# RG-LRU gate products in quarters of TensorE, adaLN weights in half transfers, and a first norm without GpSimd

## The chip, the cores and the metric

The kernel runs on one core of a Trainium2 chip. The metric is the time of one execution on the device in microseconds (us); lower is better. A core has TensorE (PE: matmuls; PEld: its weight loads, which overlap the matmuls), VectorE (DVE), ScalarE (ACT), GpSimd (POOL) and SyncE (SP), which issues the transfers. Each engine takes its instructions strictly from its own queue and waits on semaphores for the others. Times come from the median of several executions; the rows come from one profiled execution.

## The reference

Two layers of a hybrid trunk over 512 tokens (256 context, 256 latent) of width 1024. In each layer, a modulated RMS norm, one input projection, three token mixers side by side (RG-LRU, chunked GLA, attention), a gated merge, an output projection, and an MLP. What the change touches is the modulated norm and the gates of the RG-LRU:

```python
def modulate(x, g, shift, scale):
    return rms_norm(x, g) * (1 + scale) + shift

def rglru_coeffs(xc, a_w, a_b, x_w, x_b, lam):
    bn, n, w = xc.shape
    xh = xc.reshape(bn, n, LRU_BLOCKS, LRU_BLOCK_W)
    r = jax.nn.sigmoid(jnp.einsum('bnhi,hij->bnhj', xh, a_w).reshape(bn, n, w) + a_b).astype(jnp.float32)
    i = jax.nn.sigmoid(jnp.einsum('bnhi,hij->bnhj', xh, x_w).reshape(bn, n, w) + x_b)
    log_a = -RGLRU_C * r * jax.nn.softplus(-lam.astype(jnp.float32))
    a = jnp.exp(log_a)
    u = jnp.sqrt(-jnp.expm1(2.0 * log_a)) * (i * xc).astype(jnp.float32)
    return a, u
```

`xc` is the projection after a convolution over four tokens. There are two directions with weights of their own, so four products (`a_w` and `x_w`, forward and reverse) for each of LRU_BLOCKS = 16 blocks of 64 channels. `shift` and `scale` come from `c_silu @ mod_w + mod_b` (adaLN), a product with a few columns of its own for context and latent tokens.

## The kernel before, in words

Activations lie channels on partitions: eight tiles of 128 channels by 512 tokens. A projection (`gemm`, L256) of one 128-column weight tile is 24 matmuls, as weights and activations are split in a high and a low fp32r part (`weight_parts`, L194: ACT casts `wh`, DVE subtracts `wl`); in layer 1 the projections of which only the latent half is used run on 256 columns. Weight tiles of 512 KB come through `weight_raw` (L189) into three buffers, the split parts into three more, so that a load waits until DVE has split the tile three before. Matmuls on plain fp32 operands show as two records in the trace, called two passes here.

**The start** (L453 to L484). `mod_load` (L381) fetches 2 MB of `mod_w`, a quarter of what the first norm needs, in one transfer; SyncE's order is quarter, two weight tiles, quarter, one weight tile, two quarters. `mod_half` / `mod_cols` (L313) make a quarter's product in 32 fp32 matmuls of 32 output columns, four on column tiles of their own (`ps[32 * j:32 * j + 32]`), then ACT copies, PE transposes and DVE adds the bias into `modT`. `norm_stats` (L397) sums squares, and PE broadcasts the inverse root to all partitions (L417, from diagonal tiles that DVE makes, L416) into PSUM `pb`, which ACT copies to `sb`. `norm_apply` (L429) multiplies each tile: even `k` on DVE from `pb`, odd `k` on GpSimd from `sb` (L439); scale and shift on DVE for `k` in `NDVE = (0, 2, 5)` (L446), on ACT for the others (L448); `split_to` (L306) casts on ACT (L307) and subtracts on DVE (L308). The first three projections go along with it, two `k` at a time.

**The RG-LRU stage** (L692 to L721). `gate_y` (L538) is a projection and a Gelu; `lru_conv` (L548) a projection, one ACT step and three DVE steps into `xc`; `lru_gates` (L558) four fp32 matmuls 128x128x512 with block-diagonal weights `gw` (256 KB, L561), each into a PSUM tile of its own from `ps_mx` (four buffers), a Tanh each (L567), and for each direction another Tanh (L571) and a DVE product (L572). `lru_decay` is Exp (L578), L710 a Sqrt over a pair of tiles, `lru_scan` DVE's scans and the split of the result. Tiles go in pairs; LYS gives the number of `gate_y` per step (2, 2, 1, 0 behind the first three):

```python
        for i in range(0, 8, 2):
            lru_conv(i + 1)
            if i < 6:
                lru_gates(i)
                lru_conv(i + 2)
            else:
                kq0 = gla_kq(0)
                lru_gates(i)
            lru_gates(i + 1)
            for j in range(2):
                lru_decay(i + j)
            tt = ws_[1][:, i % 4:i % 4 + 2]
            S.activation(tt, tt, AF.Sqrt, scale=0.25, bias=epsc)
            for j in range(LYS[l][i // 2 + 1]):
                gate_y(next(ly))
```

The program names an order, but the framework places each engine's instructions itself: by program order and priority among what is ready in its own model of the time (weight loads have a priority 800 instructions ahead). The queues are fixed by that before the kernel runs.

Of the kernel before, what the change touches and what calls it, by code (L numbers as in the profile page):

```python
# [15 lines left out]
F32 = mybir.dt.float32  # L16
# [8 lines left out]
T = 512  # L25
# [16 lines left out]
NDVE = (0, 2, 5)  # L42
NL = 2
O_LX, O_LY, O_GQ, O_GK, O_GV, O_GR, O_GZ = 0, 1024, 2048, 2560, 3072, 4096, 5120
# [60 lines left out]
def trunk_kernel(ctx: ExitStack, tc: tile.TileContext, out: bass.AP, d: dict):  # L105
    nc = tc.nc
    V, S, G, P = nc.vector, nc.scalar, nc.gpsimd, nc.tensor
# [11 lines left out]
    sm = ctx.enter_context(tc.tile_pool(name="sm", bufs=2))  # L119
# [21 lines left out]
    def mx():  # L141
        return ps_mx.tile([128, 512], F32, name="mx")
# [40 lines left out]
    x1 = load_x()  # L183
# [5 lines left out]
    def weight_raw(*key):  # L189
        r = wraw.tile([128, 1024], F32, name="wraw")  # L190
        nc.sync.dma_start(r, d["wt"][order[key]])
        return r
# [185 lines left out]
        yield pace  # L378
        turn()

    def mod_load(l, u, h, tag):  # L381

        t = yp.tile([128, KT, 2, 256], F32, name="modw", tag=tag)
        nc.sync.dma_start(t, d["mod_w"][l, u, h].rearrange("p k (h c) -> p k h c", h=2))
        return t

    def mod_half(l, u, h, t):
# [38 lines left out]
        h = hp.tile([128, KT, 2, T], F32R, name="h")  # L426
        return (h[:, :, 0, :], h[:, :, 1, :], a, g, h)

    def norm_apply(l, which, x, c0, c1, st, hn, ks):  # L429
        n = c1 - c0  # L430
        sh0, sc0 = (0, 8) if which == 1 else (24, 32)
        hh, hl, a, g = hn[:4]
        k0, k1, s0, s1 = ks[0], ks[-1] + 1, c0 // 256, c1 // 256
        V.scalar_tensor_tensor(a[:, k0:k1, s0:s1], modT[l][:, sc0 + k0:sc0 + k1, s0:s1], 1.0, g[:, k0:k1, s0:s1],
                               op0=ALU.add, op1=ALU.mult)
        for k in ks:
            h = tmp()
            if k % 2:
                G.tensor_tensor(h[:, :n], x[:, k, c0:c1], st[1][:, :n], op=ALU.mult)  # L439
            else:  # L440
                V.tensor_tensor(h[:, :n], x[:, k, c0:c1], st[0][:, :n], op=ALU.mult)
            for s in range(s0, s1):
                c = slice(256 * s - c0, 256 * s - c0 + 256)
                sc, sh = a[:, k, s:s + 1], modT[l][:, sh0 + k, s:s + 1]
                if k in NDVE:
                    V.tensor_scalar(h[:, c], h[:, c], sc, sh, op0=ALU.mult, op1=ALU.add)  # L446
                else:
                    S.activation(h[:, c], h[:, c], AF.Identity, scale=sc, bias=sh)  # L448
            split_to(hh[:, k, c0:c1], hl[:, k, c0:c1], h[:, :n])

    hn1 = norm_mul(0, 1)  # L453
    mq = [mod_load(0, 0, 0, "yh")]
    raw = [weight_raw(0, "in", O_LY + 128 * i) for i in range(2)]
    mq.append(mod_load(0, 0, 1, "yl"))
    raw.append(weight_raw(0, "in", O_LY + 256))
    mq += [mod_load(0, 1, h, ("yh", "yl")[h]) for h in range(2)]
    first_ps = [ps_mm.tile([128, 512], F32, name="mm") for _ in range(3)]

# [8 lines left out]
    st = norm_stats(x1, 0, between=lambda: next(gs[0]))  # L469
    run(gs[0])  # L470
    next(gs[1])
    norm_apply(0, 1, x1, 0, T, st, hn1, range(2))
    run(gs[1])
    first = [weight_parts(r) for r in raw]
    for q in range(4):
        first_gemm(0, q)
        if q < 2:
            next(gs[q + 2])
        if q < 3:
            norm_apply(0, 1, x1, 0, T, st, hn1, range(2 * q + 2, 2 * q + 4))  # L480
        first_gemm(1, q)
        if q < 2:
            run(gs[q + 2])
        first_gemm(2, q)  # L484
# [30 lines left out]
    for l in range(NL):  # L515
        last = l == NL - 1
        c0 = 256 if last else 0
        n0 = T - c0
        x = x1
# [18 lines left out]
        def gate_y(i):  # L538
            if l == 0 and i < 3:
                ps = first_ps[i]  # L540
            else:
                ps = gemm(weight(l, "in", O_LY + 128 * i, hi=E_LYH), hh, hl, c0)
            ge[i] = x[:, i, :256] if last else tmp()
            S.activation(ge[i], ps, AF.Gelu_apprx_tanh)

        xcs = {}

        def lru_conv(i):  # L548
            ps = gemm(weight(l, "in", O_LX + 128 * i, hi=E_LXH, lo=E_LXL, ahead=AHEAD if l or i > 1 else 0), hh, hl, 0)
            xc = xcs[i] = tmp()  # L550

            S.activation(xc, ps, AF.Identity, scale=pc(l, "cw", 8 + i, 1), bias=pc(l, "cb", i, 1))
            x3, p3 = (a.rearrange("p (s t) -> p s t", s=2) for a in (xc, ps))
            for k, (a, b) in ((0, (1, 256)), (2, (0, 255)), (3, (0, 254))):
                V.scalar_tensor_tensor(x3[:, :, a:b], p3[:, :, a + k - 1:b + k - 1], pc(l, "cw", 8 * k + i, 1),
                                       x3[:, :, a:b], op0=ALU.mult, op1=ALU.add)

        def lru_gates(i):  # L558
            xc = xcs.pop(i)
            gw = sm.tile([128, 4, 128], F32, name="gw")  # L560
            nc.sync.dma_start(gw, d["lruw"][l, i])  # L561
            rt, tt, ix = (t[:, i % 4] for t in ws_)
            for dd in range(2):
                for q, dst in ((0, rt), (1, ix)):
                    pg = mx()
                    P.matmul(pg, gw[:, 2 * dd + q, :], xc, start=True, stop=True)  # L566
                    S.activation(dst[:, dd, :], pg, AF.Tanh, scale=0.5,  # L567
                                 bias=habx[:, l, 16 * q + 8 * dd + i:16 * q + 8 * dd + i + 1])

                c2p = c2[:, l, 1, 8 * dd + i:8 * dd + i + 1]  # L570
                S.activation(tt[:, dd, :], rt[:, dd, :], AF.Tanh, scale=c2p, bias=c2p)  # L571
                V.scalar_tensor_tensor(ix[:, dd, :], ix[:, dd, :], 1.0, xc, op0=ALU.add, op1=ALU.mult)  # L572
# [117 lines left out]
        LYS = LYS0, LYS1  # L690
        ly = iter(range(8))
# [4 lines left out]
            gate_consts()  # L696
        for i in range(0, 8, 2):
            lru_conv(i + 1)
            if i < 6:
                lru_gates(i)  # L700
                lru_conv(i + 2)
            else:

                kq0 = gla_kq(0)
# [3 lines that stand above are left out]
                lru_decay(i + j)  # L708
            tt = ws_[1][:, i % 4:i % 4 + 2]
            S.activation(tt, tt, AF.Sqrt, scale=0.25, bias=epsc)  # L710
            for j in range(LYS[l][i // 2 + 1]):
                gate_y(next(ly))
            if i == 6:
                gates0 = gla_gates(0)
                v0 = gla_v(0)
            for j in range(2):
                lru_scan(i + j)
            if i == 6:
                ys0 = gla_r(0)
            if i == GZP:  # L720
                zs = gla_z()  # L721
# [399 lines left out]
def layout(inp):  # L1121
# [52 lines left out]
        put(l, "qg", A["q_norm_g"][l])  # L1174
        put(l, "kg", A["k_norm_g"][l])
    a["par"] = par
    lruw = np.zeros((NL, 8, 128, 4, 128), f)
    for dd in range(2):
        for q, name in enumerate(("lru_a_w", "lru_x_w")):
            w = A[name][:, dd].reshape(NL, 8, 2, 64, 64)  # L1180
            for s in range(2):
                lruw[:, :, 64 * s:64 * s + 64, 2 * dd + q, 64 * s:64 * s + 64] = w[:, :, s]
    a["lruw"] = lruw
    glaw = np.zeros((NL, 3, 32, 2, 512), f)
    for dd in range(2):
# [36 lines left out]
```

## Time and profile before

| | us |
|---|---|
| median of 3 runs | 1862.1 (1861.45 to 1863.89) |
| the profiled execution | 1860.73 |
| its span, first to last instruction | 1858.9 |
| mean granted TensorE clock | 0.993 |

Groups of rows give for each line of the kernel the engine, the operation, what it writes and reads (out<-in), and the shape (partitions x elements; for matmuls also rows*columns of the weights). In timelines the first number is the start from the span's begin and the second the time from the first start to the last end, both in us; instructions of one kind are merged (xcount), and square brackets hold the engine's idle time before them and what ended it. Matmuls are pipelined, so that their records overlap: the distance between starts is what one costs. A few records can be missing.

### The profile page before, as it was taken

The page shows a single profiled execution, that of the slowest core. Times are in us where ns is not written, and L with a number is a line of the kernel's source. Part 1 is how long each engine was busy: PE and PEld are TensorE (multiplying, and loading weights), DVE is VectorE, ACT ScalarE, POOL GpSimd, SP SyncE. Part 2 cuts the span into 40 slices and gives each one's busy share as a digit, 9 for nine tenths or more (in the row PEclk, how much of TensorE's full clock was granted, in tenths as well). Part 3 has the DMA queues.
Part 4 walks back from the last instruction along what each step waited for, and adds up shares of the span by engine and source line. Part 5 has one row for each costly group of instructions (what it writes and reads, how often), then busy time and mean ns, then how long its engine had stood idle before and what let it go on. Part 6 is the DMA issues. An engine that isn't in the chain of part 4 may idle for free.

```text
span 1858.9 us, 26345 instructions
## 1 busy us (share of the span) xinstructions
PE 1803.0 (97%) x9992; PEld 1496.2 (80%) x9992; DVE 1288.0 (69%) x2206; ACT 936.3 (50%) x1620; POOL 62.8 (3%) x87
## 2 busy tenths in 40 slices
PE   5999999999999999999999999999999999999999
PEld 4766788888787888988888889767889877878887
DVE  4786775454557777789763447797876588778776
ACT  4787545333444333564332325788665455556443
POOL 1000000000000000000000000000000000000000
PEclk9999999999999999999999999999999999999999
DMA  8322222232211556666753235522333432755554
GB/s 324 102 76 85 70 82 80 70 102 80 68 57 52 196 188 201 215 219 208 237 178 100 91 95 184 173 92 85 109 101 122 131 125 91 261 170 159 186 188 148
DMA packets 82143, 255.59 MB, mean 137 GB/s; under 512 B 9184, under 2 KB 12384, under 8 KB 81248
## 3 DMA queue, kind: packets, MB, share of 16 engines
q1 hardware_dynamic: 82016, 253.90, 42.0%
q8 instruction: 79, 1.29, 0.3%
q14 instruction: 48, 0.39, 0.1%
HBM read 252.82 MB, written 1.05 MB: 137 GB/s over the span
## 4 chain that ended last, share of the span: by engine, by line
PE 59%; issue 22%; DVE 9%; ACT 7%; POOL 1%; DMA 1%; SPq 0%; POOLq 0%; DVEq 0%; ACTq 0%
PE mm L216 48%; PE mx L216 5%; DVE wl L201 2%; PE mx L841 2%; ACT lru L567 1%; PE mx L220 1%; PE mx L822 1%; ACT wh L200 1%; ACT lru L710 1%; DVE lru L586 1%; PE mx L566 1%; DVE lru L588 1%; ACT lru L571 1%; PE mx L793 1%; DMA wraw<-wt 1%
## 5 line engine op out<-in xcount | busy, mean ns | idle before, releaser
L216 PE MATMUL mm<-h,wh 128*128 128x512 f32 (+1 forms) x2512 | 729.6, 370 | 7.1 <-ACT h L307 5.1
L200 ACT CAST wh<-wraw 128x1024 fp32r<-128x1024 f32 x365 | 382.2, 1049 | 500.9 <-PE mm L216 391.5
L201 DVE TENSOR_TENSOR wl<-wraw,wh 128x1024 fp32r<-128x1024 f32 x365 | 445.5, 1222 | 235.6 <-ACT wh L200 219.9
L216 PEld LDWEIGHTS mm<-h,wh 128*128 128x128 f32 x2512 | 452.4, 189 | 91.5 <-issue 7.2
L216 PE MATMUL mm<-h,wl 128*128 128x512 f32 (+1 forms) x1448 | 493.9, 341 | 0.0
L216 PEld LDWEIGHTS mm<-h,wl 128*128 128x128 f32 x1448 | 274.0, 189 | 31.6 <-issue 1.4
L216 PE MATMUL mm<-yh,wh 128*128 128x512 f32 (+1 forms) x640 | 224.7, 351 | 2.2 <-DVE big L1039 2.1
L216 PE MATMUL mm<-yh,wl 128*128 128x512 f32 (+1 forms) x640 | 224.0, 350 | 0.0
L216 PE MATMUL mm<-yl,wh 128*128 128x512 f32 (+1 forms) x640 | 222.4, 348 | 0.0
L216 PE MATMUL mm<-yp,wh 128*128 128x512 f32 (+1 forms) x576 | 183.6, 374 | 2.5 <-ACT g L873 2.3
L216 PE MATMUL mm<-wh,h 128*128 128x512 f32 x576 | 183.4, 395 | 0.0
L216 PE MATMUL mm<-yp,wl 128*128 128x256 f32 x512 | 145.1, 283 | 0.0
L370 DVE SCALAR_TENSOR_TENSOR t<-t,cs,t 128x512 f32<-128x512 f32 x178 | 127.2, 746 | 25.6 <-DMA t<-mod_w 18.7
L216 PEld LDWEIGHTS mm<-yh,wh 128*128 128x128 f32 x640 | 121.7, 190 | 17.4 <-issue 3.0
L216 PEld LDWEIGHTS mm<-yh,wl 128*128 128x128 f32 x640 | 121.2, 189 | 15.4 <-issue 0.7
L216 PEld LDWEIGHTS mm<-yl,wh 128*128 128x128 f32 x640 | 121.2, 189 | 14.9 <-issue 0.5
L216 PEld LDWEIGHTS mm<-wh,h 128*128 128x128 f32 x576 | 107.7, 188 | 23.1 <-issue 1.0
L216 PEld LDWEIGHTS mm<-yp,wh 128*128 128x128 f32 x576 | 104.1, 189 | 24.0 <-ACT g L873 2.5
L216 PE MATMUL mm<-wl,h 128*128 128x512 f32 x288 | 113.4, 394 | 0.0
L216 PEld LDWEIGHTS mm<-yp,wl 128*128 128x128 f32 x512 | 96.9, 189 | 0.8 <-issue 0.7
L216 PE MATMUL mx<-t,t 128*128 128x128 f32 (+2 forms) x416 | 81.7, 338 | 0.1
L989 ACT ACTIVATE t<-mx,mxs,rsq 128x512 f32<-128x512 f32 (+1 forms) x48 | 33.9, 709 | 74.0 <-DVE mxs L987 72.0
(223 smaller groups left out, 2006.5 us busy)
## 6 DMA issues: line engine op xcount, KB each, us to landing
wraw<-wt SPq DMA_DIRECT2D x365, 512.0 KB, 3.6
t<-mod_w SPq DMA_DIRECT2D x144, 256.0 KB, 3.5
modw<-mod_w SPq DMA_DIRECT2D x6, 2048.0 KB, 14.4
big<-xt SPq DMA_DIRECT2D x8, 512.0 KB, 5.1
gw<-lruw SPq DMA_DIRECT2D x16, 256.0 KB, 3.7
out<-big SPq DMA_DIRECT2D x8, 128.0 KB, 1.9
t<-glaw SPq DMA_DIRECT2D x8, 96.0 KB, 2.9
t<-ropeg SPq DMA_DIRECT2D x2, 256.0 KB, 3.3
```

The costliest lines, as they stand in the source:

```text
L200: S.copy(wh, r)
L201: (G if lo == "G" else V).tensor_tensor(wl, r, wh.bitcast(F32), op=ALU.subtract)
L216: P.matmul(o, a, b, **kw)
L220: P.transpose(o, a, ident)
L370: V.scalar_tensor_tensor(a, t, c, a, op0=ALU.mult, op1=ALU.add)
L566: P.matmul(pg, gw[:, 2 * dd + q, :], xc, start=True, stop=True)
L567: S.activation(dst[:, dd, :], pg, AF.Tanh, scale=0.5, bias=habx[:, l, 16 * q + 8 * dd + i:16 * q + 8 * dd + i + 1])
L571: S.activation(tt[:, dd, :], rt[:, dd, :], AF.Tanh, scale=c2p, bias=c2p)
L586: V.tensor_tensor(u, u, h, op=ALU.mult)
L588: V.tensor_tensor_scan(h, a, u, 0.0, op0=ALU.mult, op1=ALU.add)
L841: P.matmul(po[:, :256], a, b, start=j == 0, stop=j == len(mm) - 1)
L989: S.activation(p[:, :128 * nk], psc[:, :128 * nk], AF.Exp, scale=r, bias=mxs[:, 1:2], accum_out=mxs[:, 2:3])
```

## The change

Three things. `mod_load` issues two transfers of 1 MB (`k` 0 to 3, 4 to 7) with a callback between them, and the first weight tile is now issued between the halves of the second quarter, the other two behind it. `norm_apply` gets `on_g`; with False, as the first norm calls it, all multiplies are on DVE from PSUM and all scales and shifts on ACT. `lru_gates` uses 64x64 matmuls: `gw` holds the `a` blocks on partitions 0 to 63 and the `x` blocks on 64 to 127 (128 KB), and as each block of channels needs both, `lru_conv` makes a copy `xs` of `xc` with its halves swapped, by two transfers on SyncE, in a `g2` buffer. `gate_y` moves: half of a step's go behind `lru_conv(i + 1)`, ahead of the gates, the other half behind `lru_conv(i + 2)`.

```diff
-    def mod_load(l, u, h, tag):
+    def mod_load(l, u, h, tag, between=lambda: None):
         t = yp.tile([128, KT, 2, 256], F32, name="modw", tag=tag)
-        nc.sync.dma_start(t, d["mod_w"][l, u, h].rearrange("p k (h c) -> p k h c", h=2))
+        src = d["mod_w"][l, u, h].rearrange("p k (h c) -> p k h c", h=2)
+        nc.sync.dma_start(t[:, :4], src[:, :4])
+        between()
+        nc.sync.dma_start(t[:, 4:], src[:, 4:])
         return t
...
-            if k % 2:
+            if k % 2 and on_g:
                 G.tensor_tensor(h[:, :n], x[:, k, c0:c1], st[1][:, :n], op=ALU.mult)
...
-                if k in NDVE:
+                if k in NDVE and on_g:
                     V.tensor_scalar(h[:, c], h[:, c], sc, sh, op0=ALU.mult, op1=ALU.add)
...
-    mq = [mod_load(0, 0, 0, "yh")]
-    raw = [weight_raw(0, "in", O_LY + 128 * i) for i in range(2)]
-    mq.append(mod_load(0, 0, 1, "yl"))
-    raw.append(weight_raw(0, "in", O_LY + 256))
+    raw = []
+    mq = [mod_load(0, 0, 0, "yh"),
+          mod_load(0, 0, 1, "yl", lambda: raw.append(weight_raw(0, "in", O_LY)))]
+    raw += [weight_raw(0, "in", O_LY + 128 * i) for i in range(1, 3)]
...
+            xs = xss[i] = gtmp()
+            nc.sync.dma_start(xs[:64], xc[64:])
+            nc.sync.dma_start(xs[64:], xc[:64])
...
-            xc = xcs.pop(i)
-            gw = sm.tile([128, 4, 128], F32, name="gw")
+            xc, xs = xcs.pop(i), xss.pop(i)
+            gw = sm.tile([128, 2, 128], F32, name="gw")
...
             for dd in range(2):
+                pgs = mx(), mx()
+                for q in range(2):
+                    r = slice(64 * q, 64 * q + 64)
+                    for b in range(2):
+                        P.matmul(pgs[q][64 * b:64 * b + 64, :], gw[r, dd, 64 * b:64 * b + 64],
+                                 (xc if b == q else xs)[r, :], start=True, stop=True)
                 for q, dst in ((0, rt), (1, ix)):
-                    pg = mx()
-                    P.matmul(pg, gw[:, 2 * dd + q, :], xc, start=True, stop=True)
+                    pg = pgs[q]
...
             lru_conv(i + 1)
+            n = LYS[l][i // 2 + 1]
+            for j in range(0, n, 2):
+                gate_y(next(ly))
             if i < 6:
                 lru_gates(i)
                 lru_conv(i + 2)
+                for j in range(1, n, 2):
+                    gate_y(next(ly))
...
-            for j in range(LYS[l][i // 2 + 1]):
-                gate_y(next(ly))
```

## Rows read from the trace of the kernel before

**Rows 1.** The page: busy us of each engine, share of the span, instructions.

```profile
PE 1803.0 (97%) x9992; PEld 1496.2 (80%) x9992; DVE 1288.0 (69%) x2206; ACT 936.3 (50%) x1620; POOL 62.8 (3%) x87
```

**Rows 2.** Stretches: length, busy us per engine (instructions), granted clock, DMA share, GB/s.

```profile
63.00:172.00 109.00, 106.23 (x403) 74.97 (x402) 81.72 (x113) 84.37 (x110) 0.00 (x0) 0.98 0.27 86
1188.00:1213.00 25.00, 25.00 (x117) 18.47 (x116) 16.91 (x23) 23.74 (x30) 0.00 (x0) 1.00 0.36 119
1188.00:1285.00 97.00, 92.84 (x424) 66.52 (x423) 78.94 (x120) 84.44 (x114) 0.00 (x0) 1.00 0.30 97
```

**Rows 3.** Timeline of PE around one gates call of layer 0.

```profile
62.50 0.62 PE L216 MATMUL mm<-h,wh 128*128 128x512 f32 x2
62.95 0.39 PE L216 MATMUL mm<-h,wl 128*128 128x512 f32 x1
63.18 3.60 PE L566 MATMUL mx<-t,gw 128*128 128x512 f32 x8
```

**Rows 4.** The chain of work that ended last: start, us, what.

```profile
63.34 3.43 PE mx L566 x8
```

**Rows 5.** Timeline of the start: PE, GpSimd, DVE and ACT.

```profile
12.81 1.84 PE L409 MATMUL mx<-meanc,t 128*128 128x1 f32 x8 [12.81 <-DVE t L406]
...
16.81 1.04 ACT L200 CAST wh<-wraw 128x1024 fp32r<-128x1024 f32 x1 [5.46 <-DMA wraw<-wt]
...
18.07 1.05 ACT L200 CAST wh<-wraw 128x1024 fp32r<-128x1024 f32 x1 [0.21 <-DMA wraw<-wt]
...
19.36 2.08 PE L417 MATMUL mx<-t,ones 128*128 128x128 f32 x8 [0.17 <-DVE t L416]
...
22.10 0.69 DVE L441 TENSOR_TENSOR t<-big,mx 128x512 f32<-128x512 f32 x1 [0.19 <-ACT t L419]
22.14 5.04 POOL L439 TENSOR_TENSOR t<-big,t 128x512 f32<-128x512 f32 x4 [6.20 <-ACT t L419]
...
23.52 1.09 ACT L448 ACTIVATE t<-t,modT,amul 128x256 f32<-128x256 f32 x2 [1.46 <-DVE amul L434]
23.94 2.11 DVE L446 TENSOR_SCALAR t<-t,amul,modT 128x256 f32<-128x256 f32 x2
...
26.09 0.62 ACT L307 CAST h<-t 128x512 fp32r<-128x512 f32 x1 [0.82 <-DVE t L446]
...
26.76 0.79 PE L216 MATMUL mm<-h,wh 128*128 128x512 f32 x1 [5.12 <-ACT h L307]
...
27.48 3.64 PE L216 MATMUL mx<-modw,cs 128*32 128x128 f32 x64
...
32.69 0.74 DVE L446 TENSOR_SCALAR t<-t,amul,modT 128x256 f32<-128x256 f32 x2
```

**Rows 6.** Timeline of PE around the third adaLN quarter.

```profile
35.24 0.39 PE L216 MATMUL mm<-h,wl 128*128 128x512 f32 x1
...
35.56 1.96 PE L216 MATMUL mx<-modw,cs 128*32 128x128 f32 x64
...
37.45 0.73 PE L216 MATMUL mm<-h,wh 128*128 128x512 f32 x2
```

**Rows 7.** Timeline of ACT behind the first gates call.

```profile
68.61 1.28 ACT L578 ACT_TABLE_LOAD   x1
69.90 1.52 ACT L578 ACTIVATE lru<-lru,c 128x512 f32<-128x512 f32 x2
```

**Rows 8.** Timeline of PE and of ACT at layer 0's last gates call.

```profile
163.52 0.62 ACT L307 CAST yh<-lru 128x512 fp32r<-128x512 f32 x1 [3.55 <-DVE lru L595]
...
164.78 5.40 PE L566 MATMUL mx<-t,gw 128*128 128x512 f32 x8 [2.77 <-ACT lru L567]
```

**Rows 9.** Timeline of DVE: the three steps of the first conv.

```profile
59.94 2.31 DVE L555 SCALAR_TENSOR_TENSOR t<-mm,par,t 128x510 f32<-128x510 f32 x3
```

**Rows 10.** SyncE's waits from 52 to 236 us: total us, times, longest.

```profile
SPq L191 <- DVE wl L201: 143.3, 23, 9.6
```

**Rows 11.** The page, DMA issues: count, KB each, median us from issue to landing.

```profile
gw<-lruw SPq DMA_DIRECT2D x16, 256.0 KB, 3.7
```

More of the change, by code (lines that the diff above doesn't have):

```diff
@@ L427, in norm_mul, with norm_apply @@
         return (h[:, :, 0, :], h[:, :, 1, :], a, g, h)
-    def norm_apply(l, which, x, c0, c1, st, hn, ks):
+    def norm_apply(l, which, x, c0, c1, st, hn, ks, on_g=True):
         n = c1 - c0
@@ L471, in trunk_kernel @@
     next(gs[1])
-    norm_apply(0, 1, x1, 0, T, st, hn1, range(2))
+    norm_apply(0, 1, x1, 0, T, st, hn1, range(2), False)
     run(gs[1])
@@ L479, in trunk_kernel @@
         if q < 3:
-            norm_apply(0, 1, x1, 0, T, st, hn1, range(2 * q + 2, 2 * q + 4))
+            norm_apply(0, 1, x1, 0, T, st, hn1, range(2 * q + 2, 2 * q + 4), False)
         first_gemm(1, q)
@@ L544, in gate_y @@
             S.activation(ge[i], ps, AF.Gelu_apprx_tanh)
-        xcs = {}
+        xcs, xss = {}, {}
         def lru_conv(i):
@@ L1176, in layout @@
     a["par"] = par
-    lruw = np.zeros((NL, 8, 128, 4, 128), f)
+    lruw = np.zeros((NL, 8, 128, 2, 128), f)
     for dd in range(2):
@@ L1181, in layout @@
             for s in range(2):
-                lruw[:, :, 64 * s:64 * s + 64, 2 * dd + q, 64 * s:64 * s + 64] = w[:, :, s]
+                lruw[:, :, 64 * q:64 * q + 64, dd, 64 * s:64 * s + 64] = w[:, :, s]
     a["lruw"] = lruw
```

## The prediction

> **What bounds the kernel now.** I read the busy shares first [rows 1]: PE 97%, DVE 69%, ACT 50%. These are averages, so I cut out the two stages that the change touches most, the RG-LRU stages of layer 0 (63 to 172 us) and layer 1 (1188 to 1285 us), and read each engine's busy time there [rows 2]. PE is busy for 106.2 of 109 us and 92.8 of 97 us. ACT, 50% on average, is at 84.4 of 109 and 84.4 of 97 us here, and in layer 1's first pair of channel tiles at 23.7 of 25 us. DVE stands at 81.7 and 78.9 us. So PE sets the end of these stages, but ACT is close behind it, hardly any distance at all in layer 1. Whatever PE loses, ACT can give back only up to its own busy time.
>
> Then the PE timeline around one gates call [rows 3]: behind projection matmuls, which start 0.227 us apart (three between 62.50 and 63.18), stand eight gate passes, four fp32 matmuls of two passes each. The chain of work that ended last has them at 3.43 us, 0.429 us a pass [rows 4]. There are 16 such calls (128 passes), 54.9 us in all, nearly all on the path.
>
> Last the first 50 us, by their timelines [rows 5]: PE has the norm's broadcast done at 21.4 us and starts its first projection matmul at 26.76, behind ACT's cast of a normed tile, which in turn waits for DVE's scale and shift (L446). Those two took 2.11 us while GpSimd was multiplying (22.14 to 27.18), and 0.74 us a little later without it. The second adaLN quarter runs only then, and slowly: 3.64 us where a later one takes 1.96 [rows 6]. From there on PE runs without a gap worth naming.
>
> **The gates, per call.** Before, 3.43 us. After, the same four products are eight 64x64 matmuls of two passes, one in each quarter of the array, for each direction. If all four quarters run side by side, a direction costs two passes, a call 4 x 0.429 = 1.72 us. Does the trace show tiles side by side? In columns, yes: an adaLN quarter is 32 matmuls on four 32-column tiles, 64 passes of 128 columns in 1.96 us [rows 6]. A full-width pass of 512 columns takes 0.429 us, so one of 128 about 0.107, and 64 of them in a row 6.9 us: the column tiles run 3.5 deep. In rows (partitions 0 to 63 beside 64 to 127) no row of this trace shows it. Bounds, then: 1.72 us (both), 3.43 us (columns only), 6.86 us (neither). I take 1.72, nearest to the column row. Entering and leaving the tiled form costs something: the first column pass starts 0.32 us behind the last projection matmul instead of 0.227, and the two matmuls behind it take 0.73 us instead of 0.62 [rows 3, 6]; with the start that they lose I put 0.3 us a call. So 2.0 us, a saving of 1.4 us a call, 11.2 us for each layer's eight.
>
> The Trainium skill, "TensorE: Matmul & The Clock Gate", Part 3, says that matmuls start and end strictly in program order. Taken at its word, the second pass of a tile would have to start before the first pass of the next tile, so only neighbours would overlap: 9 x 0.429 = 3.9 us a call, no gain. The column tiles speak against that: by the same rule their 64 passes would take 33 x 0.107 = 3.5 us, and the row has 1.96.
>
> **What is late next: ACT.** Two further changes load ACT. gate_y moves from behind the Sqrt to between the gates of a pair. Today a pair loads three tables of functions, for Exp, Sqrt and Gelu, at 1.28 us [rows 7]; Tanh runs behind Exp or Gelu without a load. Exp of the first tile of a pair runs ahead of the second gates' Tanh already now (its load at 68.61, the two Exp at 69.90 us, while conv 2's projection still runs). With a Gelu between the two gates, the order becomes Gelu, Exp, Gelu, Exp, Sqrt: five loads where LYS puts two gate_y's (two pairs a layer), 4 x 1.28 = 5.1 us a layer more. Bounds: 0 (if Exp isn't drawn ahead any more) and 5.1. I take 5.1, since ACT is as idle there as before while the conv's projection runs.
>
> The Trainium skill, "ScalarE: Activation LUTs", section "What ACT_TABLE_LOAD costs", puts a switch at some 2.66 us, a drain counted in. The rows disagree: the load stands at 68.61 and the next activation starts at 69.90, 1.29 us later [rows 7]. By the page's figure the sum below would be about 4 us poorer.
>
> Layer 0 [rows 2, 8]: PE would need 106.2 - 11.2 = 95 us. Its one stall, 2.8 us ahead of the last gates call with the slower passes behind it (5.40 us, and 3.60 for the call of [rows 3]), comes from ACT: the Tanh that frees the PSUM tile queues behind a cast of the scan's result, which waits for DVE. It may go, as Tanh becomes ready earlier against the scans, or grow, since one projection (5.45 us) that stands ahead of it today moves forward. ACT needs 84.4 + 5.1 = 89.5 us, 94% of PE's 95. In-order queues that full don't hide each other's waits; I take 9.5 us of the possible 11 to 15.
>
> Layer 1 [rows 2]: ACT needs 84.4 + 5.1 = 89.5 of 97 us, so no more than 7.5 us can go whatever PE does, and in the first pair ACT needs 23.7 + 2.6 = 26.3 us where the pair takes 25 today. I take 4 us. Bounds for both layers together: 27 us saved (11.2 a layer, layer 0's stall of 2.8 and the 1.8 of its slower passes, no table loads) and nothing.
>
> **The swapped copies.** Each conv tile adds two SBUF-to-SBUF transfers of 128 KB to SyncE's queue. They wait for the conv's last DVE step (2.31 us for three, [rows 9]), and all weight loads are queued behind them. SyncE waits 143.3 us for DVE to free weight buffers (23 waits from 52 to 236 us, the longest 9.6) [rows 10], so weights are fetched as early as there is room for them, and a few us lost there cost nothing. In the other direction a copy can sit behind such a wait. Landing: no transfer within SBUF is in this trace; the nearest, the gate weights' 256 KB from HBM, take 3.7 us [rows 11], and I keep that as the upper bound for half as much. ACT's first step about 1.0 + 2.3 + mean wait 6.2 + 3.7 = 13.2 us in a bad ordinary case, against a cover of two projections of 24 matmuls, 2 x 5.45 = 10.9 us (the next conv and the gate_y that now stands ahead of the gates). Since SyncE takes its queue in the order in which things become ready, I cost it at nothing; where the bad case holds it costs the difference, 2.3 us a call, and without the cover of gate_y 7.8. The g2 buffers (four) suffice for three copies and wzs. The halved gate weights (128 KB for 256) were not waited for.
>
> **The start** [rows 5]. Half transfers: 0.5 MB lands every 1.26 us (ACT's casts of the first two weight tiles wait for them until 16.81 and 18.07), so the first weight tile comes 1 MB or 2.5 us later (19.3 us), the second adaLN quarter, with one weight tile less ahead of it, 1.3 us earlier, and the first quarter's matmuls can begin on its first half. They then start when PE has the sums of squares (12.81 + 1.84 = 14.65 us), so a quarter of 3.64 us ends at 18.3, and the broadcast of the norm, today from 19.36 to 21.44, up to 1 us earlier, at 20.5. Without GpSimd, DVE's multiply is 0.69 us and nothing slows it; ACT scales in 1.09 and casts in 0.62 us. First matmul: 20.5 + 0.7 + 0.3 (the modulation's small steps, an estimate) + 1.1 + 0.6 = 23.2 us instead of 26.76. If the second quarter fills the idle time ahead of it, up to 2.5 us more. ACT then needs 1.7 us for each of eight tiles, 3.4 for two, under PE's 18 x 0.227 = 4.1 us of matmuls for two; DVE's four more multiplies (4 x 0.69) stand against six scales less (3 x 0.74). Bounds: 7 us gained, 2 us lost (if the diagonal tiles on DVE still queue behind the first weight's split, now 2.5 us later). I take 4.5.
>
> **Sum.** 4.5 + 9.5 + 4 = 18 us. From the profiled run's 1860.7 us (span 1858.9) that gives 1842.7; the median of the runs shown is 1862.1, 1.4 above, so 1844.
>
> **Rivals.** (a) ACT isn't the limit: the loads are not added, the stall goes; 27 + 4.5 us: 1831. For it: ACT has idle time in layer 0. Against: 23.7 of 25 us in layer 1. Chance 0.12. (b) Row halves don't overlap, columns do: 3.43 + 0.3 us a call, 16 x 0.3 = 4.8 us lost, 4.5 won at the start, ACT's loads 1 to 2 us in layer 1: 1864. No row shows row halves side by side, and none shows a limit on them. 0.11. (c) Slower: no quarter overlaps another, as the passes of one instruction hold the array: 6.86 + 0.3 - 3.43 = 3.7 us a call, 60 us over 16: 1917. It decides as soon as a direction takes more than four passes in a row. The column row speaks against it: 0.04. (d) Slower: the copies come late. From 10.9 us behind the projection's end PE waits; at 3 us for 14 of the calls 42 us: 1886. It decides at 18 / 14 = 1.3 us a call. 0.06. (e) The order by which the first in, first out queues are filled turns out worse at the start and ACT eats the rest: within 0.2%: 0.05.
>
> **How the numbers follow.** The forecast has 0.62, its own range 1834 to 1856. 0.2% is 3.7 us, about what a measurement of this kernel can tell from no change. Faster: 0.61 + 0.12 + 0.02 (of b, e) = 0.75. Same: 0.13. Slower: 0.12. For 8 in 10 the range takes in half of (a) and most of (b): 1830 to 1864.
>
> **What would show it.** Right: a gates call at about 2 us with its passes in groups of four; Gelu loads twice a pair; ACT over 90% busy in both stages; the first projection matmul by 24 us. Wrong: gates calls of 3.4 us or more (rows don't overlap), PE waiting for a transfer ahead of the gates (d), or PE stalls on ACT's Tanh longer than 2.8 us.

## The result and the profile after

The changed kernel takes 1880.2 us (median of 4 runs, 1875.1 to 1881.0) against 1861.8 in the runs beside it: a ratio of 1.0094 (95% interval 1.0072 to 1.0116), 17.5 us slower where 18 us faster was forecast. Its profiled execution has a span of 1878.0 us. The page's line on engines answers [rows 1]; under it the stretches of [rows 2] (columns as there), with one of 12 us from 110 us on between them.

```profile
PE 1807.7 (96%) x10120; PEld 1486.0 (79%) x10120; DVE 1286.3 (68%) x2204; ACT 948.3 (50%) x1633; POOL 62.7 (3%) x83
```

```profile
63.00:172.00 109.00, 100.42 (x437) 65.40 (x435) 70.99 (x96) 81.74 (x101) 0.00 (x0) 0.94 0.31 89
110.00:122.00 12.00, 10.76 (x26) 4.22 (x26) 6.24 (x9) 5.40 (x7) 0.00 (x0) 0.57 0.44 127
1188.00:1285.00 97.00, 91.28 (x466) 62.59 (x465) 72.56 (x110) 77.81 (x107) 0.00 (x0) 0.98 0.43 126
```

In layer 0's stage every engine is less busy than in [rows 2] and the granted clock is 0.94 for 0.98: nothing got fuller, the engines wait for each other more. ACT, forecast at over 90%, is busy for 75% of it. (The third row has the times of [rows 2], but layer 1's first gates call starts at 1203.1 us here and at 1188.4 before, so it isn't the same work.) Marks in the trace show where the time went: on VectorE the 31st split of a weight, which lies behind layer 0's stage, starts 10.5 us later than before (257.2 for 246.6), the 236th, behind layer 1's stage, 21.1 us later, and the 305th, behind the last layer's adaLN, 18.9. So each layer loses some 10 us and the last adaLN gives 2 back.

The first gates call shows that the quarters do what they are for. PE's timeline, which answers [rows 3]:

```profile
67.33 0.39 PE L216 MATMUL mm<-h,wl 128*128 128x512 f32 x1
67.65 0.64 PE L578 MATMUL mx<-t,gw 64*64 64x512 f32 x1
67.65 0.65 PE L578 MATMUL mx<-g,gw 64*64 64x512 f32 x2
67.67 1.05 PE L578 MATMUL mx<-t,gw 64*64 64x512 f32 x2
68.13 0.60 PE L578 MATMUL mx<-g,gw 64*64 64x512 f32 x2
...
69.00 0.59 PE L578 MATMUL mx<-t,gw 64*64 64x512 f32 x1
69.52 0.73 PE L216 MATMUL mm<-h,wh 128*128 128x512 f32 x2
70.10 0.39 PE L216 MATMUL mm<-h,wl 128*128 128x512 f32 x1
```

Sixteen passes start in four groups 0.43 to 0.48 us apart. From the last `wl` matmul ahead of the call to the first one behind it (two `wh` matmuls lie between, too) it is 2.77 us, 67.33 to 70.10; in the kernel before it is 4.12 us, from 62.95 in [rows 3] to the row below. So a whole call saves 1.35 us.

```profile
67.07 0.39 PE L216 MATMUL mm<-h,wl 128*128 128x512 f32 x1
```

But only 8 of the 16 calls stand whole in PE's trace. The fourth call of layer 0 looks otherwise (PE):

```profile
106.27 0.39 PE L216 MATMUL mm<-h,wl 128*128 128x512 f32 x1
111.25 1.93 PE L578 MATMUL mx<-t,gw 64*64 64x512 f32 x2 [4.59 <-ACT yh L307]
113.11 1.22 PE L216 MATMUL mm<-h,wh 128*128 128x512 f32 x2
...
115.97 1.97 PE L578 MATMUL mx<-g,gw 64*64 64x512 f32 x2
117.86 1.22 PE L216 MATMUL mm<-h,wh 128*128 128x512 f32 x2
...
119.86 1.11 PE L578 MATMUL mx<-g,gw 64*64 64x512 f32 x1
119.87 1.12 PE L578 MATMUL mx<-t,gw 64*64 64x512 f32 x2
```

Three things are to be seen. PE stands still for 4.6 us ahead of the call. The call is split: a product on xc, then projection matmuls, then one on the copy (tile g), then projections again; only from 119.86 on do quarters run together. And all of it runs slowly: the granted clock is 0.57 from 110 to 122 us, a lone quarter pass takes some 0.9 us.

The row puts the wait down to ACT's cast of yh, which ends at about the same moment (110.52 + 0.62 = 111.14) but isn't read by these matmuls. What they read is t, the conv's result; behind ACT's row, DVE's and SyncE's timelines show when that is there:

```profile
110.52 0.62 ACT L307 CAST yh<-lru 128x512 fp32r<-128x512 f32 x1 [3.13 <-DVE lru L610]
```

```profile
104.92 0.74 DVE L558 SCALAR_TENSOR_TENSOR t<-mm,par,t 128x510 f32<-128x510 f32 x1
105.58 0.68 DVE L605 TENSOR_TENSOR_SCAN lru<-lru 128x256 f32<-128x256 f32 x1
...
109.14 0.74 DVE L558 SCALAR_TENSOR_TENSOR t<-mm,par,t 128x510 f32<-128x510 f32 x1
109.80 0.68 DVE L610 TENSOR_TENSOR lru<-lru,t 128x512 f32<-128x512 f32 x1
110.40 0.74 DVE L558 SCALAR_TENSOR_TENSOR t<-mm,par,t 128x508 f32<-128x508 f32 x1
```

```profile
111.17 0.47 SPq L563 DMA_DIRECT2D g<-t  x1
111.69 0.59 SPq L564 DMA_DIRECT2D g<-t  x1
```

The conv's three DVE steps, 2.31 us in a row in [rows 9], are strung out among the scans of the pair before and end at 111.1 us; only then are the copies issued, and PE can start on xc but not on the copy. That the program's order on PE splits the call there is the same thing seen from PE: products on xc become ready before those on the copy, and projections were put between. Waits that name a copy come to only 1.1 us in this trace.

### The profile page after: what moved, and what is told of

It is laid out like the page before. It is cut to its first block, busy times and chain, and to the rows that moved or that the text cites. A ratio compares the mean times of both kernels' runs of the same rounds, so it can differ in the third digit from the quotient of the medians.

```text
span 1878.0 us, 26688 instructions
## 1 busy us (share of the span) xinstructions
PE 1807.7 (96%) x10120; PEld 1486.0 (79%) x10120; DVE 1286.3 (68%) x2204; ACT 948.3 (50%) x1633; POOL 62.7 (3%) x83
## 4 chain that ended last, share of the span: by engine, by line
PE 29%; issue 20%; DVE 4%; ACT 3%; DMA 1%; POOL 0%; POOLq 0%; SPq 0%; ACTq 0%; DVEq 0%
PE mm L216 25%; PE mx L216 2%; DVE wl L201 1%; ACT wh L200 1%; PE mx L859 1%; PE mx L840 1%; PE mx L220 0%; PE mx L578 0%; ACT lru L730 0%; DVE lru L601 0%; DVE lru L603 0%; DMA g<-t 0%; ACT lru L593 0%; DMA wraw<-wt 0%; POOL t L442 0%
```

## The experiments

All ratios are to the kernel before, timed beside the run, with the 95% interval; "us" behind one is the ratio taken of 1862 us. Profiled executions differ in one stretch that no edit touches: the last 60 weight tiles take 175.8 to 180.6 us between their issues, and 164.8 us in half of the traces and 167.9 in the others between their splits. So stages are compared by marks inside the trace, and of each kernel there is one trace.

**The parts one by one.** First the change cut into its three parts, and all of it but the moved gate_y. *Start alone:*

> The kernel before with the start alone: half transfers, the first weight tile between them, and the first norm without GpSimd; gates and gate_y as before. In the changed kernel's trace the first gates call stands at 67.65 us with one projection (5.45 us) more ahead of it than before (63.18), so the start gains about 1 us there; near the end, after the adaLN halves of the last layer, the lag behind the kernel before falls from 20.9 to some 18.5 us. All theories: 1858 to 1861 us against 1861.8.

*Quarters and copies alone* (gate_y and the start as before):

> The kernel before with the gates in quarters and the swapped copies alone; start and gate_y as before. Theory 'cover' (the moved gate_y takes away the two projections that hid the scans behind the Sqrt): without the move the saving on PE comes through in part, 1848 to 1856 us. Theory 'copies' (the swapped copies come late and tear the calls apart): the first gates of a pair now have one projection of cover in place of two, so worse than the changed kernel: 1878 to 1895 us. Theory 'tables' (the added function tables on ACT): no table is added here, so 1845 to 1855.

*gate_y moved alone:*

> The kernel before with the moved gate_y alone; gates in full matmuls, no copies, start as before. Theory 'cover': slower by about what the changed kernel lost and what its quarters gained, 1875 to 1890 us. Theory 'copies': no difference, 1860 to 1864. Theory 'tables': eight more loads of 1.28 us, in part on the path, 1865 to 1872.

*All of the change, gate_y put back:*

```diff
-            n = LYS[l][i // 2 + 1]
-            for j in range(0, n, 2):
-                gate_y(next(ly))
...
+            for j in range(LYS[l][i // 2 + 1]):
+                gate_y(next(ly))
```

> The changed kernel with gate_y back behind the Sqrt: quarters, copies and the start stay. Theory 'cover': 1846 to 1855 us, the quarters-only time less 1 to 3 for the start. Theory 'copies': 1876 to 1893. Theory 'tables': 1843 to 1853.

Measured: start 0.9984 [0.997, 0.9998], -3.0 us; quarters 1.0068 [1.0052, 1.0085], +12.7; gate_y 1.0039 [1.0022, 1.0055], +7.3; all but gate_y 1.0084 [1.0065, 1.0104], +15.6. The three sum to +17.0, close to the whole, but not in pairs: start and quarters together are 5.9 us worse than their sum, and gate_y costs only 1.9 more on top of them (intervals of 5 us on both figures). The quarters, from which (with gate_y's loads counted in) 13.5 us were forecast, are the greater part of the loss.

**What the quarters lose.** Three edits of the quarters-only kernel (e2): one without the copies, which leaves out the swap, so that half of the gates are of the wrong channels; one with every call whole; and that one with the conv raised in priority against the scans as well.

```diff
-            xs = xss[i] = gtmp()
-            nc.sync.dma_start(xs[:64], xc[64:])
-            nc.sync.dma_start(xs[64:], xc[:64])
+            xss[i] = xc
```

> The quarters alone as in e2 (gate_y behind the Sqrt, start of before), but without the swapped copies: all four quarters read xc itself, so half of the two gates are taken from the wrong 64 channels (that swap is the part left out) and no DMA and no wait on one is left. PE then writes 15 of the 16 gates calls whole. Theories for the 12 us that e2 loses: TORN (e2's order on PE splits 4 of 16 calls at a point where the matmuls on xc are ready and those on the copy are not, each split call costs some 3 us of lone passes and switches, the calls that stay whole gain their 1.3 us): 1844 to 1852 us. LATE (PE stands still for copies that come in late, the copies are issued late because the conv steps stand behind scans on VectorE): 1844 to 1852 too, since both are gone. SPEED (the quarters themselves give nothing on this path: ScalarE and VectorE set the gates stage, and they have more work in their way): 1860 to 1872 us.

```diff
-            nc.sync.dma_start(xs[64:], xc[:64])
+            last_copy[i] = nc.sync.dma_start(xs[64:], xc[:64])
...
+                        tc.add_manual_dep(m.ins, last_copy[i].ins.name, ...Sync...)
```

> e2 with each of the eight matmuls of a call made to wait for the second copy, so that PE's order holds them together: 15 of 16 calls whole, copies kept, none earlier. TORN: 1854 to 1863 us, the 12 us that e2 loses are gone. LATE: 1872 to 1882 us, as e2 or worse, since all eight now wait for the copy. SPEED: 1868 to 1876, no change against e2.

```diff
+            with tc.high_priority(300):
                 S.activation(xc, ps, AF.Identity, ...)
...
                 nc.sync.dma_start(xs[:64], xc[64:])
```

> e6 with the conv steps on ScalarE and VectorE and the copies raised in priority, so that they go ahead of the scans of the pair before: copies come earlier, calls whole. LATE: 1850 to 1864 us, at least 6 us under e6. TORN: within 3 us of e6. SPEED: 1866 to 1878, no gain against e6.

Measured: no copies 1.0012 [0.9998, 1.0025], +2.2 us; whole calls 1.0041 [1.0026, 1.0056], +7.6; whole calls with the conv first 1.0055 [1.0033, 1.0076], +10.2. Whole calls gain about 5.1 us against e2, taking the copies away about another 5.4 (intervals of 4 us on each; together 10.5). In e2's trace 4 of the 16 calls have projection matmuls among theirs, in e6's and e5's one. No theory had both right: TORN forecast that whole calls would win everything back, LATE that they would win nothing and that the conv first would win at least 6 us, where it won nothing. And e5 is the surprise: whole calls, no transfer, no wait on one, and still no gain, which SPEED alone had forecast. Its trace says where the shorter calls went (PE, then DVE and ACT):

```profile
154.74 1.95 PE L573 MATMUL mx<-t,gw 64*64 64x512 f32 x16
163.80 4.40 PE L573 MATMUL mx<-t,gw 64*64 64x512 f32 x16 [7.12 <-ACT lru L577]
```

```profile
161.35 0.67 DVE L605 TENSOR_TENSOR lru<-lru,t 128x512 f32<-128x512 f32 x1
...
162.05 0.62 ACT L307 CAST yh<-lru 128x512 fp32r<-128x512 f32 x1 [5.46 <-DVE lru L605]
162.58 0.59 ACT L677 ACTIVATE t<-mm 128x512 f32<-128x512 f32 x1
163.07 1.26 ACT L577 ACTIVATE lru<-mx,par 128x512 f32<-128x512 f32 x2
```

PE has the seventh call done at 156.7 us and waits 7.1 us for the Tanh that frees its PSUM tiles. That Tanh is queued on ACT behind the cast of a scan's result, and the cast waits 5.5 us for DVE. It is the stall of [rows 8], 2.8 us there; PE, faster now, arrives 5.3 us earlier and starts the last call only 1.0 us earlier (163.80 for 164.78). And the call behind it takes 4.40 us instead of 1.95, at a granted clock of 0.54 (158 to 172 us):

```profile
158.00:172.00 14.00, 8.20 (x25) 4.26 (x26) 8.53 (x13) 9.91 (x16) 0.00 (x0) 0.54 0.34 95
```

**The casts behind the Tanh.** If that queue is what gives the gain back, then putting the cast behind the next pair's Tanh must free it, with and without the quarters.

```diff
-            split_to(y1h[:, i, c0:], y1l[:, i, c0:], y)
+            casts[i] = S.copy(y1h[:, i, c0:], y)
+            V.tensor_tensor(y1l[:, i, c0:], y, y1h[:, i, c0:].bitcast(F32), op=ALU.subtract)
...
+                    tc.add_manual_dep(casts[i - 2].ins, tanh.ins.name, ...NoSync...)
```

On the kernel before:

> Before, with one edit: on ScalarE the cast of each scan's result (which waits for VectorE's scans) is queued behind the gates' Tanh of the next pair, no longer ahead of it. Theory CHAIN: the end of each RG-LRU stage is set by the chain conv, gates, Exp, Sqrt, scans, cast, and ScalarE's queue, taken in order, hands VectorE's lateness on to the Tanh that frees PSUM for the gates; PE's stall there (2.8 us in layer 0 and 3.0 in layer 1) and the lower granted clock behind it go: 1852 to 1858 us. Theory QUEUE-FREE (the cast is only the last of several things that are late; the stall stays and is put down to something else): 1859 to 1864 us.

On e6, the whole calls with copies:

> e6 (whole gates calls, copies, gate_y behind the Sqrt) with the casts queued behind the next pair's Tanh. CHAIN: the time that the quarters save on PE was given back in that queue, so this is 6 to 15 us under e6: 1850 to 1861 us. Theory COPIES (the copies alone hold PE up; the 5.4 us between e5 and e6 are theirs, and so is the clock that falls behind each stall): 1864 to 1869 us, as e6.

On e5, without copies:

> e5 (quarters that read xc alone; the swap of halves is left out, so half of the gates are of the wrong channels) with the casts behind the next pair's Tanh. CHAIN: 1845 to 1855 us, the 11 to 13 us that the quarters save on PE show at last. COPIES: as e5, 1860 to 1865 us, as the copies had already gone there.

Measured: before 0.9962 [0.9949, 0.9975], -7.1 us; whole calls with copies 1.005 [1.0033, 1.0067], +9.3, no gain against e6; without copies 0.9963 [0.995, 0.9976], -6.9, which is 9 us under e5. CHAIN holds wherever no copy is waited for; in e6 PE's waits at the gates of layer 0 are for copies (11.5 us in three) and none for a Tanh, so the edit has nothing to free there. But the quarters without copies are still no faster than the kernel before with the same edit. In layer 0 they are, by 4.7 us at the 31st weight split; layer 1 gives a part of it back (2.7 us from the 181st to the 236th), and PE's, then DVE's rows of e12 show how:

```profile
1264.16 0.40 PE L216 MATMUL mm<-wl,h 128*128 128x512 f32 x1
1269.86 1.13 PE L574 MATMUL mx<-t,gw 64*64 64x512 f32 x4 [5.30 <-issue]
```

```profile
1265.39 0.74 DVE L556 SCALAR_TENSOR_TENSOR t<-mm,par,t 128x510 f32<-128x510 f32 x1
...
1267.78 0.74 DVE L556 SCALAR_TENSOR_TENSOR t<-mm,par,t 128x510 f32<-128x510 f32 x1
...
1269.04 0.72 DVE L556 SCALAR_TENSOR_TENSOR t<-mm,par,t 128x508 f32<-128x508 f32 x1
```

The conv's last step ends at 1269.76 and PE starts at 1269.86: again conv steps among scans.

**The conv raised in priority as well.** The edit of e7 on the three kernels above: on e9,

> e9 (before, casts of the scans behind the next pair's Tanh) with the conv steps on ScalarE and VectorE raised in priority, so that they go ahead of scans that stand interleaved with them. Theory ORDER (what is left of the stalls comes from the order of the in-order queues: in e9 1.2 and 2.5 us in layer 1): 1850 to 1854 us. Theory FULL (in layer 1 ScalarE and VectorE have no room, so an order only moves the lateness): 1853 to 1857 us, as e9.

on e10,

> e10 (whole calls, copies, casts later) with the conv steps and the copies raised in priority, so that the copies start earlier. ORDER: 5 to 15 us under e10, 1853 to 1864 us. FULL: 1866 to 1872 us. Theory COPIES (a copy's way, semaphore, queue, transfer, wait, is longer than what covers it even if the conv is in time): 1862 to 1869 us.

and on e12,

> e12 (quarters that read xc alone, the swap of halves left out; casts later) with the conv steps raised in priority. In e12 the 4.6 us that layer 0 gained against e9 were given back in layer 1, by stalls of 2.9 and 5.7 us behind conv steps that stand among scans. ORDER: those go, 1842 to 1850 us. FULL: 1853 to 1857 us, as e12.

Measured: before 0.9962 [0.9945, 0.998], -7.1 us, no change against e9; with copies 1.0007 [0.9994, 1.0021], +1.3, 8 us better than e10; without copies 0.9943 [0.9925, 0.9961], -10.6. What is left to the quarters with all known obstacles away, and the swap left out, is 3.5 us against e13, with an interval of 5: not shown to be a gain. With the same orders the copies cost 12 us (e14 against e15). Layer 0, from 60 us to the end mark at the 31st split of a weight (in this order: before, after, e5, e13, e14, e15):

```profile
60.00:246.60 186.60, 179.17 (x740) 135.13 (x739) 137.06 (x199) 133.09 (x185) 2.45 (x5) 0.98 0.26 82
60.00:257.20 197.20, 181.38 (x801) 130.06 (x800) 137.30 (x198) 138.61 (x189) 3.84 (x5) 0.94 0.28 82
60.00:247.60 187.60, 172.12 (x798) 128.57 (x797) 135.85 (x196) 132.62 (x185) 2.40 (x5) 0.94 0.24 74
60.00:240.60 180.60, 175.41 (x734) 133.40 (x733) 136.28 (x197) 132.19 (x185) 4.18 (x5) 0.99 0.26 82
60.00:245.00 185.00, 170.36 (x798) 126.52 (x797) 136.79 (x197) 132.39 (x185) 3.85 (x5) 0.96 0.29 86
60.00:236.10 176.10, 167.26 (x803) 126.19 (x802) 136.98 (x198) 131.84 (x185) 3.85 (x5) 0.99 0.25 79
```

The granted clock carries much of the loss. The part of the clock not granted is 0.02 x 186.6 = 3.7 us before and 0.06 x 197.2 = 11.8 after, 8 us more, within the rounding of the clock's last digit (about 1 us each); in e15 it is 1.8 us. PE's idle time, the stretch less its busy time, is 7.4 us before and 15.8 after, 8.4 us more. Of these 16 us the quarters' shorter work gives back some 6, and 10.6 are lost. (About 1 us of what the changed kernel isn't granted falls where PE stands idle anyway.) The copies' part of the standing still is seen best in e14: they hold PE up for 8.1 us in layer 0 (waits of PE: total, times, longest), and one copy's way reads as follows on DVE, SyncE and PE:

```profile
PE mx L577 <- DMA g<-t: 8.1, 3, 4.8
```

```profile
97.24 0.71 DVE L557 SCALAR_TENSOR_TENSOR t<-mm,par,t 128x508 f32<-128x508 f32 x1
```

```profile
98.03 0.47 SPq L562 DMA_DIRECT2D g<-t  x1
98.55 0.59 SPq L563 DMA_DIRECT2D g<-t  x1
```

```profile
100.99 1.08 PE L577 MATMUL mx<-t,gw 64*64 64x512 f32 x1 [4.82 <-DMA g<-t]
```

From the end of the conv's last step, 97.95, to PE's first pass it is 3.0 us: two issues of 0.5 us in a row, then the transfer (128 KB, 2.3 us from issue to landing on the changed kernel's page). The conv's three steps still stand among scans here, from 94.72 us on, in spite of the priority. In layer 1 the gain doesn't come even without copies. The stage of layer 1, each from some 5.5 us behind its first gates call, e13 and then e15:

```profile
1188.60:1286.00 97.40, 97.21 (x449) 71.63 (x448) 76.70 (x117) 86.99 (x115) 0.00 (x0) 1.00 0.30 95
1184.00:1281.00 97.00, 90.76 (x492) 64.64 (x491) 76.63 (x117) 86.53 (x115) 0.00 (x0) 0.96 0.28 84
```

PE's work is 6.5 us less and the stage as long, and PE's idle time takes the clock to 0.96. ACT is busy for 87 of 97 us in both, but that ACT holds the stage is not shown. From the 181st to the 236th weight split, which take in layer 1's stage and what follows it, the kernel before takes 277.0 us, e13 278.7, e15 and e5 280.6, and e16 of the next paragraph, in which ACT has five table loads and 6.6 us less to do there, 279.8. Neither less work on PE nor less on ACT made it shorter. (With whole calls and copies it is 283.5 to 285.9, e14, e6 and e7, in the changed kernel 287.2.) So FULL has the outcome of layer 1 right and ORDER that of layer 0; what holds layer 1 stays open.

**gate_y: tables or cover.** Tanh in place of gate_y's Gelu, which then needs no table load beside Exp's:

```diff
-            S.activation(ge[i], ps, AF.Gelu_apprx_tanh)
+            S.activation(ge[i], ps, AF.Tanh)
```

> Before with Tanh in place of gate_y's Gelu (the part changed: the multiplier of the RG-LRU branch is another function), as the ground for the next run. Tanh needs no function table of its own behind Exp, Gelu does. A load less ahead of each Gelu that follows the Sqrt is replaced by one for Tanh, so 1858 to 1863 us by both theories.

> e3 (only gate_y moved, 5.7 us slower than before) with Tanh in place of Gelu, so that the moved gate_y need no load between the two Exp. Theory TABLES (the loads are what e3 loses): within 2 us of the run of before with Tanh. Theory COVER (two projections stood behind the Sqrt and hid scans; moved, they hide nothing): 4 to 8 us above it.

Measured: before with Tanh 0.9972 [0.9957, 0.9988], -5.2 us, a gain that neither theory had forecast; moved, 0.9997 [0.9984, 1.0009], -0.6. The gain has a plain candidate: with Gelu the kernel before has three loads a pair in layer 0, with Tanh two. gate_y's move costs 4.7 us with no table load added (e16 and e17 both have two a pair), against 7.3 with them: more than the 2 us of TABLES and within COVER's 4 to 8. But the difference, 2.6 us, can't be called the price of the loads: the intervals are 3 to 4 us on each figure, and the marks show two different losses. At the 31st weight split the move has cost 1.1 us with Gelu and 4.6 with Tanh; from the 181st to the 236th it costs 6.8 with Gelu and 0.3 with Tanh. That the lost cover behind the Sqrt is the cause, and not the new order of the queues, is argued and not shown. The loads themselves are there in the changed kernel: where the kernel before has Exp's [rows 7], the Sqrt's and the Gelu's behind it, a pair now has Exp's at 72.81 us, the moved Gelu's, Exp's again and the Sqrt's (ACT):

```profile
81.57 1.28 ACT L547 ACT_TABLE_LOAD   x1
...
87.20 1.28 ACT L593 ACT_TABLE_LOAD   x1
...
90.97 1.28 ACT L730 ACT_TABLE_LOAD   x1
```

**The start.** Only the half transfers (also the last layer's), and the start on top of two other kernels, e10 and e13:

> Of the change at the start only the adaLN quarters in halves with the weights among them (these halves are used in the last layer too); the first norm still on GpSimd and VectorE. e1, which has the norm too, gained 3.7 us, and its trace showed the gain behind the last layer's adaLN quarters and a loss of 1 us behind the start. Theory HALVES (the gain is the last layer's): 1857 to 1860 us. Theory NORM (the gain is from the norm without GpSimd): 1861 to 1865 us.

> e10 with the start of the changed kernel (norm without GpSimd, adaLN quarters in halves). If the start's 3.7 us of e1 are its own: e10 less 2 to 4 us, 1847 to 1858 by CHAIN. If the order of the queues decides anew each time (theory LOTTERY: e4 lost 6 us more than e1 and e2 add up to): anywhere within 6 us of e10, above it as well.

> Before with what helped: the changed kernel's start, the casts of the scans behind the next pair's Tanh and the conv steps ahead of the scans; gates as before, whole and without copies. If the start's gain in e1 adds to that of e13: 1850 to 1854 us. LOTTERY (the start changes the order downstream): 1853 to 1858 us.

Measured: halves alone 1.0005 [0.9995, 1.0016]; start on e10 1.0021 [1.001, 1.0033], 5.4 us better than e10; on e13 0.9956 [0.9938, 0.9974], -8.2 us, 1.1 better than e13. With e1 (-3.0) and e4 against e2 (+2.9) the same edit measures from -5.4 to +2.9 us. Only these two ends lie apart by more than their intervals (4 and 5 us), which is as far as LOTTERY is shown. HALVES is wrong in its time and right in its place: from the 271st to the 305th weight split, with the last layer's adaLN, the six kernels with half transfers take 122.3 to 124.0 us and the others 124.7 to 126.1. What e8 loses against that stands at the start: its first gates call comes at 65.11 us, that of e1, with the norm, at 63.35, that of the kernel before at 63.18. So the halves lose 1.9 us there and the norm without GpSimd wins 1.8 back. e18, the kernel before with the new start, the casts behind the Tanh and the conv first, has at 1852.15 us the lowest median of the kernels that leave nothing out; by their intervals it can't be told from e9 and e13. It beats the kernel before and the changed kernel.

## Why the prediction was wrong

**The calls: right in themselves.** Four quarters run side by side; a saving of 1.4 us a call was forecast, and 1.35 measured where a call is whole. Row halves do overlap, so rivals (b) and (c) fall. The Trainium skill, "TensorE: Matmul & The Clock Gate", Part 3, read pass by pass, would have given 3.9 us a call; the trace, with the first passes of four quarters together and then their second, decides against that reading.

**"I cost it at nothing": the step that failed first.** The copies were set against a cover of two projections, on the ground that SyncE takes its queue as things become ready. It does: it issues them within 0.1 us of the conv's end. What was late was DVE. The step counted the conv's three DVE steps as 2.31 us in a row, and the trace has them strung out over 6.2 us among scans (104.92 to 111.14). The cover, too, was counted by the order in the source; the program's order on PE put the calls elsewhere and split half of them. Price: about 5 us for split calls (e2 to e6) and 5.4 for the copies (e6 to e5), 12 between e14 and e15. Rival (d) named the late copies, at a chance of 0.06, with PE waiting for them; in the changed kernel PE waits for copies for 1.1 us and half of the calls are split instead, and the price of 42 us was far too high.

**The terms of 9.5 and 4 us: the step that failed by itself.** Without copies and with one call split they came to a loss of 2.2 us (e5), where a gain of 13.5 was forecast. The sum let PE's saving through because ACT's busy time still fitted into PE's. In layer 0 what sets the end is not busy time but the order in the in-order queues, Tanh behind a cast behind scans: that edit alone is worth 9 us on e5 (e12). The text saw that stall, 2.8 us in [rows 8], said that it "may go, or grow", and put no price on growing: in e5 it grew to 7.1, and the slower clock behind it cost more. (In the changed kernel itself the last call waits 1.5 us; the long stalls stand ahead of the fourth call, 4.6 us, and the sixth, 2.7.) Freed (e15 against e13), layer 0 gains 4.5 us of the 9.5 and layer 1 nothing of the 4. "ACT is close behind" may be why, but 6.6 us less of ACT's work did not shorten layer 1 either, so its cause stays open.

**gate_y: mis-sized.** The sum had four loads a layer for it, 5.1 us of ACT's time, and nothing else; e3's trace has the four in layer 0 and three in layer 1, and the move measured 7.3 us, 4.7 of them still there when no load was added. That two projections had stood behind the Sqrt, where DVE scans, was in no term; whether that is the rest is not shown.

**The start: near by luck.** First projection matmul at 24.25 us where 23.2 was forecast. The sum lacked one step: ACT's cast of the first weight tile stands in the same queue, 1.03 us, and PE waits for that. The rows, PE's and then ACT's:

```profile
24.25 0.73 PE L216 MATMUL mm<-h,wh 128*128 128x512 f32 x2 [3.84 <-ACT wh L200]
```

```profile
23.17 1.03 ACT L200 CAST wh<-wraw 128x1024 fp32r<-128x1024 f32 x1
```

The whole measured -3.0 us (e1) where -4.5 was forecast, but not where it was forecast: e1's first gates call comes 0.2 us later than before and its 31st weight split 1.1 us later, so the earlier first matmul was gone by then. What its trace gains is 1.9 us at the last layer's adaLN, which no term had, and 3.1 in the last 60 tiles, where traces differ by that much whatever the edit.

**The clock** was in the sum only as 1.8 us of slow passes that might go. The long stalls of e5 and of the changed kernel were paid for twice, once standing and once in slow passes.

What stays open: why start and quarters together are 5.9 us worse than their sum (if they are, with an interval of 5), what holds layer 1, and what gate_y's move costs beside the loads.

## What to carry to other kernels

Before taking a saving on the busiest engine at its face, look at the next instruction that this engine waits for and ask what is queued ahead of its releaser; here an edit of that queue's order alone won 7 us, and a saving of some 7 us of PE's work a layer won nothing by itself. An operand that comes by another way than its sibling (a copy beside its original) can split a packed group of matmuls unless the program holds them together, and it is late by its producer's lateness, with its own way of some 3 us on top. And a wait's named releaser is worth a second look: ahead of the split call the row named a cast that only ended at the same moment as the conv step that PE waited for.

## What the runs showed of the hardware

- Eight fp32 matmuls on 64x64 quarters, sixteen passes of 512 columns, run as four groups of four, 0.43 to 0.48 us a group, about the price of one full-width pass; at the lower granted clock some 0.9 us a group, and as much where one quarter runs alone.
- Behind a PE stall the granted clock stands near the lower of its two levels, 1.2 for 2.4 GHz, for some time: 0.57 from 110 to 122 us behind 4.6 us, 0.54 from 158 to 172 us with a stall of 7.1 in it. In layer 0 the clock not granted came to 8 us more in the changed kernel than in the kernel before.
- A swap of halves within SBUF, two transfers of 128 KB, is 3.0 us from the end of the producer to the consumer's first pass in the call of e14 shown above.
